# Retention in a written order, with four query blocks inside, padded keys and states, and scores a chunk ahead

## The chip, the cores and the metric

The kernel runs on one core of a Trainium2 chip. The metric is the device time of one execution in microseconds, as the median of several runs. A core has TensorE (PE in the profile), which multiplies matrices and writes to PSUM; VectorE (DVE), ScalarE (ACT) and GpSimd (POOL) for everything else; and SyncE (SP), whose queue issues nearly all DMAs here. Each engine works through its own list of instructions in order and waits on semaphores for the others.

## The reference, cut to what matters

The model is two blocks of two layers each. The change lies in the first layer of the second block, whose mixer splits one projection of the normed input into retention (queries, keys, values), a second attention (stick breaking, with queries `sq`, keys `sk`, values `sv`) and gates. Retention, for 1024 positions, 4 heads of 64 query and key channels and 128 value channels, in 8 chunks of 128:

```
q = rotary(q);  k = rotary(k) * dk ** -0.5
scores  = einsum('bhnid,bhnjd->bhnij', qc, kc) * decay
o_intra = einsum('bhnij,bhnje->bhnie', scores, vc)
chunk_kv = einsum('bhnjd,hj,bhnje->nbhde', kc, k_decay, vc)
step(state, kv): return state * g_chunk + kv, state      # a scan over the chunks
o_inter = einsum('bhnid,hi,nbhde->bhnie', qc, q_decay, r_prev)
out = o_intra + o_inter        # then normalised over each head's 128 channels
```

## The kernel before

All of it is f32. A dense product is three matmuls for each of eight row tiles: weights and activations are split into a high and a low part (`whi`, `wlo`, `ah`, `al`), and high by high, high by low and low by high are added up in PSUM. A block of 128 output channels by 512 positions is 24 matmuls of 512 columns (line 209); the projections that put positions on the partitions (line 221) use 256 columns. A weight block of 256 columns comes in four DMAs of 256 KB into two buffers `wraw`; ScalarE makes `whi`, GpSimd makes `wlo`, and there are two buffers for each of these, so that a block is loaded while the one before it is in use. The retention's own products are plain f32 matmuls; each is two instructions in the trace.

A scheduler orders the instructions of each engine: it goes by the order of the program text, lets later work pass where its simulation finds an engine idle, and `later()` puts work behind all other. PSUM has eight banks of 512 f32 columns: one (`f`) is held for the whole program, and the pool `psum2` of this stage has the other seven, as two double tiles `d` and three single tiles `s`.

`e2` first projects queries and keys of the retention (`both`, 8 blocks in two halves of 512 positions), which VectorE scales on their way out of PSUM (line 1405) and turns by `rope_swap`: four small DMAs that swap halves, a product on GpSimd (L410) and two on VectorE (L411, L412). Then come the values in two blocks (`tok_proj`, emptied by ScalarE, L1371), and `retention`. For each chunk j it computes, on TensorE:

- the scores of four heads, each with 64 rows of the array, the two heads of a tile in separate double-bank halves (L1465); VectorE multiplies them by the decay into `ret_a` (L1467)
- two transposes of the keys (L1472), which VectorE scales into `ret_kt` (L1473)
- for each head the values by `ret_a` (128 rows, L1483) and then, into the same columns, the state `rst` by the scaled queries `ret_q` (64 rows, L1485)
- the new state, two products of 256 columns (L1488), which VectorE adds to the old one, 64 rows by 128 columns at a time (L1493).

ScalarE copies the output over the values (L1497) and squares it (L1499), VectorE sums the squares (L1501). After chunks 3 and 7 VectorE computes 1/sqrt from the sums in nine small steps and scales four chunks (L1509); TensorE transposes them, 16 transposes into four banks (L1514), ScalarE copies each bank out (L1516) and a DMA writes it to `m_scr`.

Behind the retention, under `later()`, come the query, key and value blocks of the second attention (`qkv_proj`): four blocks of `sq`, four of `sk`, then `sv`. The weights of the first two blocks are loaded before the retention ends. One block of `sk` goes to bank `f` and can so be computed inside the retention.

Of the kernel before, what the change touches and what calls it, by code (L numbers as in the profile page):

```python
# [14 lines left out]
AF = mybir.ActivationFunctionType  # L15
ALU = mybir.AluOpType
AX = mybir.AxisListType.X
# [3 lines left out]
P = 128  # L21
# [3 lines left out]
EPS = 1e-6  # L25
# [17 lines left out]
class Kern:  # L43
# [461 lines left out]
    def e1_start(self):  # L505
# [8 lines left out]
        def vectors():  # L514
# [8 lines left out]
            self.silu_c()  # L523
        X, R = {}, {}

# [863 lines left out]
    def e2(self, act):  # L1389
        nc, A, V = self.nc, self.A, self.nc.vector  # L1390
        sq_scr, sk_scr = self.dram("sq_scr", [512, T]), self.dram("sk_scr", [512, T])
        sv_scr, g_scr, m_scr = self.dram("sv_scr", [T, 512]), self.dram("g3_scr", [1024, T]), self.dram("m3_scr", [1024, T])
        self.open_psum("2", "s", d=2, s=3)
        w_in = A["even_w_in_2"]
        sm = self.open("e2s", side="right")
        qp = self.open("retq", side="left")
        cos, sin = self.const("cos_ret", qp), self.const("sin_ret", qp)
        RQ, RK = ([self.t(qp, [P, T], nm=f"r{e}{i}") for i in range(2)] for e in "qk")
        rp = self.open("ret", side="left")

        def rev(lst):
            def evac(i, c, ps):
                a, b = CH[c]
                o = lst[i][:, a:b]
                V.tensor_tensor(o, ps, self.rbc[c], ALU.mult)
                self.rope_swap(rp, o, 2, 32, cos[:, a:b], sin[:, a:b], 512)
            return evac
        self.both(act, (rev(RQ), rev(RK)), self.w_next)
        RV = [self.t(rp, [P, 512], nm=f"rv{j}") for j in range(8)]
        for b in range(2):  # L1410
            self.tok_proj(self.wblk(w_in, 512 + b * 256, 256), act, lambda j: (RV[j][:, b * 256:(b + 1) * 256], None))
# [36 lines left out]
        return mix  # L1448

    def retention(self, rp, RQ, RK, RV, m_scr):  # L1450
# [4 lines left out]
        R = [self.t(rp, [P, P], nm=f"rst{i}") for i in range(2)]  # L1455
        ss, ms, rr = (self.t(rp, [P, 32], nm=n) for n in ("ret_ss", "ret_ms", "ret_r"))
        eo = lambda t: t.rearrange("p (e i x) -> p e i x", e=2, i=4)[:, :, 0:2, :]
        nat = lambda t: t.rearrange("p (i e x) -> p e i x", i=2, e=2)
        col = lambda h: slice((h % 2) * 512 + (h // 2) * P, (h % 2) * 512 + (h // 2) * P + P)
        for j in range(8):  # L1460
            js = slice(j * P, (j + 1) * P)
            s = self.dps()
            for h in range(4):
                r = slice(64 * (h % 2), 64 * (h % 2) + 64)
                mm(s[:, col(h)], RK[h // 2][r, js], RQ[h // 2][r, js], start=True, stop=True)  # L1465
            a = self.t(rp, [P, 512], tag="ret_a", bufs=2)
            V.tensor_tensor(nat(a), eo(s), nat(dec.rearrange("p h i -> p (h i)")), ALU.mult)  # L1467
            if j < 7:
                kt = self.t(rp, [P, 256], tag="ret_kt", bufs=2)
                s = self.sps()  # L1470
# [4 lines left out]
            o = self.dps()  # L1475
            if j:
                qd = self.t(rp, [P, 2, P], tag="ret_q", bufs=2)
                for i in range(2):
                    V.tensor_tensor(qd[:, i], RQ[i][:, js], qdec[:, i], ALU.mult)
            for h in range(4):  # L1480
                hs = slice(h * P, (h + 1) * P)
                r = slice(64 * (h % 2), 64 * (h % 2) + 64)
                mm(o[:, col(h)], a[:, hs], RV[j][:, hs], start=True, stop=j == 0)  # L1483
                if j:
                    mm(o[:, col(h)], qd[r, h // 2], R[h // 2][r], start=False, stop=True)  # L1485
            for i in range(2 if j < 7 else 0):
                d = self.sps()
                mm(d[:, 0:256], kt[:, i * P:(i + 1) * P], RV[j][:, i * 256:(i + 1) * 256], start=True, stop=True)  # L1488
                for e in range(2):
                    r = slice(64 * e, 64 * e + 64)  # L1490
                    kv = d[r, e * P:(e + 1) * P]
                    if j:
                        V.scalar_tensor_tensor(R[i][r], R[i][r], g[2 * i + e], kv, ALU.mult, ALU.add)  # L1493
                    else:
                        V.tensor_copy(R[i][r], kv)
            ot = RV[j]
            nc.scalar.activation(out=nat(ot), in_=eo(o), func=AF.Copy)  # L1497
            sq = self.t(rp, [P, 512], tag="ret_s", bufs=2)
            nc.scalar.activation(out=sq, in_=ot, func=AF.Square)  # L1499
            f = slice(4 * j, 4 * j + 4)  # L1500
            V.reduce_sum(ss[:, f], sq.rearrange("p (h e) -> p h e", h=4), axis=AX)  # L1501
            if j % 4 < 3:
                continue
            f = slice(4 * j - 12, 4 * j + 4)
            V.tensor_scalar(ms[:, f], ss[:, f], 1.0 / P, EPS, ALU.mult, ALU.add)
            self.rsqrt(rr[:, f], ms[:, f], 16)
            for u in range(j - 3, j + 1):
                ov = RV[u].rearrange("p (h e) -> p h e", h=4)
                V.tensor_tensor(ov, ov, rr[:, 4 * u:4 * u + 4].unsqueeze(2).to_broadcast([P, 4, P]), ALU.mult)  # L1509
            c = j // 4  # L1510
            for i in range(4):
                s = self.sps()
                for e in range(4):
                    nc.tensor.transpose(s[:, e * P:(e + 1) * P], RV[c * 4 + e][:, i * P:(i + 1) * P], self.ident)  # L1514
                t = self.stg()
                nc.scalar.activation(out=t, in_=s, func=AF.Copy)  # L1516
                self.dma(m_scr[i * P:(i + 1) * P, c * 512:(c + 1) * 512], t)
# [619 lines left out]
```

## Time and profile before

| | us |
|---|---|
| median of three runs (2606.64, 2608.9, 2610.66) | 2608.9 |
| the profiled execution | 2611.92 |
| its span, first to last instruction on the core | 2610.1 |
| the retention, from its first scores to its last transpose | 1610.78 to 1674.26 |
| four `sq` blocks behind it, up to the first `sk` block in bank `e` | 1674.26 to 1698.20 |

The profile gives, for each engine, the time in which it worked and the share of the span; for TensorE also the granted clock (PEclk, 1.00 is 2.4 GHz, 0.50 is 1.2 GHz). A wait is the idle time just before an instruction and is put down to the instruction that ended it. The start-to-start distance of matmuls is their price; the single times beside them are longer, because matmuls overlap.

### The profile page before, as it was taken

The numbers are of one execution on the slowest core, as the hardware profiler recorded it, in microseconds if no ns is written. First come the engines' busy times: TensorE is split into PE (matmuls) and PEld (weight loads), VectorE is DVE, ScalarE is ACT, GpSimd is POOL, SyncE is SP. The second block draws the span as 40 slices with busy tenths as digits, with TensorE's granted clock in tenths as the row PEclk, the third lists the DMA queues.
The fourth block names the chain that finished last, engine by engine and source line by source line (L and its number), as shares of the span: only waits on it lengthen the run. The fifth ranks groups of instructions, "written<-read, shape, count | busy, mean of one in ns | idle before, by whom it ended". The sixth has DMA issues, their size and how long they took to land.

```text
span 2610.1 us, 36065 instructions
## 1 busy us (share of the span) xinstructions
PE 2446.2 (94%) x12842; PEld 1967.3 (75%) x12842; DVE 1686.4 (65%) x2977; ACT 1118.6 (43%) x2169; POOL 899.0 (34%) x750
## 2 busy tenths in 40 slices
PE   5999999999999989999898989899999999999998
PEld 3887777777678876766576779687877777799888
DVE  6785437787845467777785653347788476673455
ACT  4412226666643225655464322135656333513331
POOL 4214243454411243332321413045552243453231
PEclk7999999999999999999899999899999999999999
DMA  7475431132333222221323522133233332201433
GB/s 239 134 224 190 155 102 56 51 104 74 99 107 124 73 89 61 68 73 54 95 83 97 178 68 72 55 107 106 85 108 119 100 110 89 72 22 54 163 104 101
DMA packets 217092, 265.16 MB, mean 102 GB/s; under 512 B 42768, under 2 KB 142768, under 8 KB 216784
## 3 DMA queue, kind: packets, MB, share of 16 engines
q1 hardware_dynamic: 216192, 262.75, 32.1%
q8 instruction: 101, 1.65, 0.3%
q14 instruction: 79, 0.65, 0.1%
q10 hardware_dynamic: 720, 0.10, 0.0%
HBM read 188.60 MB, written 71.97 MB: 100 GB/s over the span
## 4 chain that ended last, share of the span: by engine, by line
PE 60%; DVE 14%; DMA 10%; issue 8%; ACT 4%; POOL 4%; SPq 1%; DVEq 0%; POOLq 0%; ACTq 0%
PE s L209 9%; PE g L209 6%; PE f L209 4%; PE p L209 4%; PE s L221 4%; PE o L209 2%; DMA wmt<-in_w_modT 2%; PE t L209 2%; PE e L209 2%; PE g L1917 1%; DVE wmj L474 1%; DVE pl L166 1%; DMA mixg<-gate_scr 1%; PE o L1255 1%; PE o L958 1%
## 5 line engine op out<-in xcount | busy, mean ns | idle before, releaser
L166 POOL TENSOR_TENSOR wlo<-wraw,whi 128x512 fp32r<-128x512 f32 (+3 forms) x229 | 317.9, 1400 | 588.2 <-ACT whi L158 526.3
L158 ACT ACTIVATE whi<-wraw 128x512 fp32r<-128x512 f32 (+3 forms) x261 | 154.0, 612 | 359.0 <-PE s L209 82.9
L166 DVE TENSOR_TENSOR pl<-pf,ph 128x512 fp32r<-128x512 f32 (+1 forms) x328 | 254.4, 776 | 79.1 <-ACT pf L953 40.1
L209 PE MATMUL s<-ah,whi 128*128 128x512 f32 (+1 forms) x472 | 190.6, 404 | 13.2 <-DVE hf L1699 3.7
L209 PE MATMUL s<-al,whi 128*128 128x512 f32 (+1 forms) x472 | 189.3, 401 | 2.1 <-DVE al L492 1.4
L209 PE MATMUL s<-ah,wlo 128*128 128x512 f32 (+1 forms) x472 | 189.0, 401 | 0.6 <-POOL wlo L166 0.6
L953 ACT ACTIVATE ph<-s 128x512 fp32r<-128x512 f32 (+1 forms) x176 | 101.4, 576 | 107.5 <-PE s L950 106.7
L915 DVE TENSOR_REDUCE mx<-p 128x1 f32<-128x512 f32 (+1 forms) x208 | 116.9, 575 | 35.1 <-PE p L914 34.1
L1250 ACT ACTIVATE ph<-s 128x512 fp32r<-128x512 f32 x152 | 90.6, 596 | 112.8 <-PE s L1242 59.5
L209 PE MATMUL g<-ah,whi 128*128 128x512 f32 (+1 forms) x312 | 122.2, 392 | 3.2 <-DVE mixg L382 3.2
L209 PE MATMUL g<-ah,wlo 128*128 128x512 f32 (+1 forms) x312 | 121.7, 390 | 0.0
L209 PE MATMUL g<-al,whi 128*128 128x512 f32 (+1 forms) x312 | 121.5, 390 | 0.0
L209 PEld LDWEIGHTS s<-ah,whi 128*128 128x128 f32 x472 | 90.2, 191 | 39.2 <-issue 5.4
L209 PE MATMUL f<-ah,whi 128*128 128x512 f32 x288 | 116.2, 404 | 0.5 <-ACT accq L371 0.5
L209 PE MATMUL f<-ah,wlo 128*128 128x512 f32 x288 | 116.1, 403 | 0.0
L209 PE MATMUL f<-al,whi 128*128 128x512 f32 x288 | 115.8, 402 | 0.0
L209 PEld LDWEIGHTS s<-al,whi 128*128 128x128 f32 x472 | 90.4, 191 | 24.4 <-DVE al L492 2.1
L209 PEld LDWEIGHTS s<-ah,wlo 128*128 128x128 f32 x472 | 90.1, 191 | 22.6 <-issue 1.4
L1588 DVE TENSOR_TENSOR_SCAN scu<-scu,ones_col 128x128 f32<-128x128 f32 (+3 forms) x64 | 97.5, 1537 | 14.3 <-ACT scu L1584 12.3
L1210 DVE CUSTOM_DVE_ANT_0 p<-p,maskt 128x384 f32<-128x384 f32 (+1 forms) x128 | 67.4, 530 | 59.2 <-PE p L1209 59.1
L953 ACT ACTIVATE pf<-s 128x512 f32<-128x512 f32 (+1 forms) x176 | 100.9, 573 | 1.5 <-DVE pl L166 1.4
L474 DVE CUSTOM_DVE_ANT_0 wmj<-wmt,srow,c_b_mod 128x1024 bf16<-128x1024 f32 x56 | 76.8, 1371 | 29.1 <-DMA wmt<-in_w_modT 27.8
(756 smaller groups left out, 7490.5 us busy)
## 6 DMA issues: line engine op xcount, KB each, us to landing
wmt<-in_w_modT SPq DMA_DIRECT2D x32, 512.0 KB
wraw<-in_even_w_in SPq DMA_DIRECT2D x56, 256.0 KB
wraw<-in_odd_w_in SPq DMA_DIRECT2D x48, 256.0 KB
wraw<-in_o_w_in SPq DMA_DIRECT2D x40, 256.0 KB
xold<-x_scr SPq DMA_DIRECT2D x40, 256.0 KB
mraw<-in_w_mod SPq DMA_DIRECT2D x16, 512.0 KB
x_scr<-x SPq DMA_DIRECT2D x32, 256.0 KB
mixx<-m_scr SPq DMA_DIRECT2D x30, 256.0 KB
```

The costliest lines, as they stand in the source:

```text
L158: nc.scalar.activation(out=out, in_=in_, func=AF.Copy)
L166: return e.tensor_tensor(out, in_, hi.bitcast(F32), ALU.subtract)
L209: self.nc.tensor.matmul(out, ws[:, k, c:c + m], a[k][ch], start=first and i == j == 0, stop=last and i == len(ks) - 1 and j == 2)
L221: self.nc.tensor.matmul(out, s[k][ch][:, a:a + P], ws[:, k, c:c + n], start=first and e == i == 0, stop=last and e == len(ks) - 1 and i == 2)
L474: V.tensor_tensor_reduce(out=junk, in0=w, in1=s[:, i], scale=0.5, scalar=self.bm[l][:, m, i:i + 1], op0=ALU.mult, op1=ALU.add, accum_out=s ...
L915: V.reduce_max(mx[:, e, j:j + 1], d[:, 0:y - x], axis=AX)
L953: nc.scalar.activation(out=t, in_=s, func=AF.Exp, scale=MLA_SCALE)
L958: mm(o[0:66, 0:n], vh[:, j, :], ph, start=first, stop=False)
L1210: V.tensor_tensor_reduce(out=d[:, 0:n], in0=d[:, 0:n], in1=self.mask[:, off:off + n], scale=1.0, scalar=-3.0e38, op0=ALU.add, op1=ALU.max, ...
L1250: nc.scalar.activation(out=t, in_=s, func=AF.Exp, scale=0.125)
L1255: mm(o[0:66], vh[:, j, kv, :], ph, start=first, stop=False)
L1588: V.tensor_tensor_scan(out=rev, data0=rev, data1=self.ones.to_broadcast([P, n]), initial=1.0, op0=ALU.mult, op1=ALU.mult)
```

## The change

- The PSUM pool becomes `a`, `o` and `s` with two single tiles each and one `e`; the projections use the seven in turn ("saoe").
- The first weight block of `sq` is loaded in program order, and its four blocks become a generator `beside`, which yields after each row tile (three matmuls, 32 steps in all). `retention` draws from it: 2 steps after the first scores, 3 in every chunk, the rest after the last chunk. `qkv_proj` leaves this block out.
- `in_order` ties each TensorE instruction traced within the retention to the one before it, so that TensorE keeps the order of the text. Other work can still go between.
- Scores: ScalarE copies each key half into a tile `KZ` of two 128-column parts whose other half of the rows is zero (L1478), and the scores use all 128 rows (L1480). They are computed a chunk ahead. The tiles are cleared once on VectorE (L1463).
- States: `rst` has 128 rows by two 128-column parts, with zeros in the other halves; values by `ret_a` come first for all four heads (L1520), and then two products of 256 columns add the states (L1522).
- `norm` stands after chunks 3 and 7 as before; the transposes of the first four chunks come after chunk 5 and those of the last four at the end (`turn`, L1496, L1498).

```
-        self.open_psum("2", "s", d=2, s=3)
+        self.open_psum("2", "s", a=2, o=2, s=2, e=1)
...
-        self.both(act, (rev(RQ), rev(RK)), self.w_next)
+        self.both(act, (rev(RQ), rev(RK)), self.w_next, "saoe")
...
-        self.retention(rp, RQ, RK, RV, m_scr)
+        w, ev = self.wblk(w_in, 1536, 256), self.scaled(sq_scr)
+
+        def beside():
+
+            for c in (0, 1):
+                for i in (0, 1):
+                    yield from self.dense_steps(w, i * P, act, c, "ef", lambda ps: ev(i, c, ps))
+        with self.in_order():
+            self.retention(rp, RQ, RK, RV, m_scr, beside())
...
-                for c0, scr in ((1536, sq_scr), (2048, sk_scr)):
+                for c0, scr in ((1536, sq_scr), (2048, sk_scr))[1 - b:]:
...
-        with self.later():
-            for _ in range(2):
-                next(qkv)
...
+        R = [self.t(rp, [P, 2, P], nm=f"rst{i}") for i in range(2)]
+        KZ = [[self.t(rp, [P, 2, P], nm=f"rkz{b}{i}") for i in range(2)] for b in range(2)]
+        for t in R + KZ[0] + KZ[1]:
+            V.memset(t, 0.0)
...
+        def scores(j):
+            js = slice(j * P, (j + 1) * P)
+            s = self.sps("a")
+            for i in range(2):
+                kz = KZ[j % 2][i]
+                for e in range(2):
+                    r = slice(64 * e, 64 * e + 64)
+                    nc.scalar.activation(out=kz[r, e], in_=RK[i][r, js], func=AF.Copy)
+                for e in range(2):
+                    mm(s[:, (2 * i + e) * P:(2 * i + e + 1) * P], kz[:, e], RQ[i][:, js], start=True, stop=True)
+            A[j] = self.t(rp, [P, 512], tag="ret_a", bufs=2)
+            V.tensor_tensor(A[j], s, dec.rearrange("p h i -> p (h i)"), ALU.mult)
...
+        scores(0)
+        fill(2)
         for j in range(8):
...
             if j < 7:
+                scores(j + 1)
...
+            fill(3)
+            o = self.sps("o")
             for h in range(4):
                 hs = slice(h * P, (h + 1) * P)
-                r = slice(64 * (h % 2), 64 * (h % 2) + 64)
-                mm(o[:, col(h)], a[:, hs], RV[j][:, hs], start=True, stop=j == 0)
-                if j:
-                    mm(o[:, col(h)], qd[r, h // 2], R[h // 2][r], start=False, stop=True)
+                mm(o[:, hs], A[j][:, hs], RV[j][:, hs], start=h == 0, stop=j == 0 and h == 3)
+            for i in range(2 if j else 0):
+                mm(o[:, i * 256:(i + 1) * 256], qd[:, i], R[i].rearrange("p e x -> p (e x)"), start=False, stop=i == 1)
...
+            if j % 4 == 3:
+                norm(j // 4)
+            if j == 5:
+                turn(0)
+        fill(32)
+        turn(1)
```

On TensorE, in the middle of the retention (chunk 3), the list before has the scores of the chunk (`d_16036`, queries by keys), the two key transposes, and then values and state in turn, a pair for each head, of which the first is shown:

```order
L1465 MATMUL d_16036<-rq_3718_15185,rk_3720_15187 128x128 x2
L1465 MATMUL d_16036<-rq_3719_15186,rk_3721_15188 128x128 x2
L1472 MATMUL s_16044<-c_ident,rk_3720_15187 128x128
L1472 MATMUL s_16044<-c_ident,rk_3721_15188 128x128
L1483 MATMUL d_16048<-rv_3741_15467,ret_a_16041 128x128
L1485 MATMUL d_16048<-rst_3774_15930,ret_q_16049 128x128
```

In the list after, TensorE has in the same chunk the end of the three dense steps (`f_16092`, a query block), the values of all four heads, two state products, two products for the new state, and the scores of chunk 5 (`a_16182`):

```order
L209 MATMUL f_16092<-ah_14705,whi_15924 128x512
L209 MATMUL f_16092<-al_14706,whi_15924 128x512
L209 MATMUL f_16092<-ah_14705,wlo_15925 128x512
L1520 MATMUL o_16149<-rv_3741_15467,ret_a_16082 128x128 x4
L1522 MATMUL o_16149<-rst_3780_15948,ret_q_16137 128x256
L1522 MATMUL o_16149<-rst_3781_15949,ret_q_16137 128x256
L1525 MATMUL s_16156<-rv_3741_15467,ret_kt_16132 128x256
L1525 MATMUL s_16160<-rv_3741_15467,ret_kt_16132 128x256
L1480 MATMUL a_16182<-rq_3718_15185,rkz_3784_15952 128x128 x2
L1480 MATMUL a_16182<-rq_3719_15186,rkz_3785_15953 128x128 x2
```

The values and states no longer alternate, and between the scores of a chunk and their use lies a whole chunk.

At the end of the retention TensorE's list before goes from the last values and states (`d_16233`, chunk 7) straight to the transposes of the normalised values `rv`:

```order
L1483 MATMUL d_16233<-rv_3745_15471,ret_a_16231 128x128
L1485 MATMUL d_16233<-rst_3775_15931,ret_q_16234 128x128
L1483 MATMUL d_16233<-rv_3745_15471,ret_a_16231 128x128
L1485 MATMUL d_16233<-rst_3775_15931,ret_q_16234 128x128
L1514 MATMUL s_16263<-c_ident,rv_3742_15468 128x128
L1514 MATMUL s_16271<-c_ident,rv_3742_15468 128x128
L1514 MATMUL s_16279<-c_ident,rv_3742_15468 128x128
```

In the list after, 18 matmuls of the last query block and 24 of a key block (`f_16505`) stand there first; this is the end of the key block on TensorE:

```order
L209 MATMUL f_16505<-ah_14714,wlo_16460 128x512
L209 MATMUL f_16505<-ah_14723,whi_16459 128x512
L1496 MATMUL s_16421<-c_ident,rv_3742_15468 128x128
L209 MATMUL f_16505<-al_14724,whi_16459 128x512
L209 MATMUL f_16505<-ah_14723,wlo_16460 128x512
L1496 MATMUL s_16421<-c_ident,rv_3743_15469 128x128
L1496 MATMUL s_16421<-c_ident,rv_3744_15470 128x128
L1496 MATMUL s_16421<-c_ident,rv_3745_15471 128x128
```

The key block that filled the first chunks before has moved to this place.

On SyncE's queue, ahead of the value projection, the list before has the third part of the value weights (`wraw_15482`) ahead of the rope copies of the first half's queries (`rope_s`):

```order
L128 DMA wraw_15482<-in_even_w_in 128x2x256
L128 DMA rope_s_15218<-rq_3718_15185 32x512 x4
L128 DMA rope_s_15252<-rq_3719_15186 32x512 x4
L128 DMA wraw_15486<-in_even_w_in 128x2x256
L128 DMA wraw_15700<-in_even_w_in 128x2x256
```

In the list after, on the same queue, the third part comes behind these copies and the fourth (`wraw_15486`) behind those of the keys as well:

```order
L128 DMA rope_s_15218<-rq_3718_15185 32x512 x4
L128 DMA rope_s_15252<-rq_3719_15186 32x512 x4
L128 DMA wraw_15482<-in_even_w_in 128x2x256
L128 DMA rope_s_15286<-rk_3720_15187 32x512 x4
L128 DMA rope_s_15320<-rk_3721_15188 32x512 x4
L128 DMA wraw_15486<-in_even_w_in 128x2x256
```

The copies have moved ahead of the weights on the queue.

## Rows read from the trace of the kernel before

**Rows 1.** The page, part 1: busy us, share of the span, instructions
```profile
PE 2446.2 (94%) x12842; PEld 1967.3 (75%) x12842; DVE 1686.4 (65%) x2977; ACT 1118.6 (43%) x2169; POOL 899.0 (34%) x750
```

**Rows 2.** Stretches: us, busy us and count of each engine, PEclk, DMA share
```profile
core 0: us, PE busy (x) PEld busy (x) DVE busy (x) ACT busy (x) POOL busy (x), PEclk, DMA share, GB/s
...
1549.80:1563.60 13.80, 10.74 (x47) 8.49 (x46) 6.16 (x16) 3.01 (x5) 8.67 (x6) 0.88 0.48 136
...
1610.78:1674.26 63.48, 54.80 (x284) 40.82 (x283) 31.75 (x87) 15.96 (x28) 5.05 (x4) 0.85 0.13 42
...
1674.26:1698.20 23.94, 23.11 (x98) 18.26 (x96) 2.83 (x5) 1.73 (x4) 0.67 (x2) 0.98 0.22 82
```

**Rows 3.** TensorE's waits, 1610 to 1675: total us, times, longest
```profile
PE s L1514 <- DVE rv L1509: 4.9, 2, 4.7
...
PE d L1483 <- DVE ret_a L1467: 2.6, 3, 1.1
...
PE s L1488 <- DVE ret_kt L1473: 0.6, 1, 0.6
...
PE s L1514 <- ACT stg L1516: 0.5, 2, 0.3
```

**Rows 4.** Timeline, TensorE: start us, us, line, operation, count
```profile
1612.51 1.05 PE L1483 MATMUL d<-rv,ret_a 128*128 128x128 f32 x8
...
1613.49 0.71 PE L1465 MATMUL d<-rq,rk 64*128 64x128 f32 x8
...
1614.13 1.13 PE L1488 MATMUL s<-rv,ret_kt 128*128 128x256 f32 x4
...
1615.10 0.38 PE L1472 MATMUL s<-c_ident,rk 128*128 128x128 f32 x2
...
1628.06 0.49 PE L1483 MATMUL d<-rv,ret_a 128*128 128x128 f32 x2
...
1628.48 0.48 PE L1485 MATMUL d<-rst,ret_q 64*128 64x128 f32 x2
...
1649.83 1.12 PE L1514 MATMUL s<-c_ident,rv 128*128 128x128 f32 x4 [0.26 <-ACT stg L1516]
...
1650.74 0.63 PE L1472 MATMUL s<-c_ident,rk 128*128 128x128 f32 x2
```

**Rows 5.** Chain of waits in time, 1600 to 1720: start us, us, what
```profile
1710.71 5.61 PE f L209 x24
```

**Rows 6.** Timeline, VectorE, one chunk and the normalisation
```profile
1629.01 0.49 DVE L1479 TENSOR_TENSOR ret_q<-rq,c_ret_qdec 128x128 f32<-128x128 f32 x2 [4.26 <-PE d L1485]
...
1629.63 1.24 DVE L1493 SCALAR_TENSOR_TENSOR rst<-rst,s 64x128 f32<-64x128 f32 x4
...
1630.90 0.69 DVE L1467 TENSOR_TENSOR ret_a<-d,c_ret_dec 128x512 f32<-128x512 f32 x1
...
1631.51 0.41 DVE L1473 TENSOR_TENSOR ret_kt<-s,c_ret_kdec 128x256 f32<-128x256 f32 x1
...
1631.84 0.68 DVE L1501 TENSOR_REDUCE ret_ss<-ret_s 128x4 f32<-128x512 f32 x1
...
1669.66 2.50 DVE L1509 TENSOR_TENSOR rv<-rv,ret_r 128x512 f32<-128x512 f32 x4
```

**Rows 7.** Groups by shape, ScalarE: busy us, mean ns, idle before
```profile
L1271 ACT ACTIVATE gatt<-o 64x256 f32<-64x256 f32 x64 | 24.1, 377 | 1.2
```

**Rows 8.** Stretches of 2 us, columns as in rows 2
```profile
1642.00:1644.00 2.00, 2.00 (x10) 1.55 (x12) 0.00 (x0) 0.00 (x0) 0.00 (x0) 0.50 0.00 0
...
1654.00:1656.00 2.00, 2.00 (x14) 1.45 (x14) 1.07 (x2) 0.38 (x1) 0.00 (x0) 1.00 0.54 189
```

**Rows 9.** TensorE's waits, 1549 to 1611
```profile
PE s L209 <- DVE rq L1405: 2.2, 1, 2.2
...
PE f L369 <- DVE rt L351: 0.9, 1, 0.9
```

**Rows 10.** Timeline, SyncE's queue
```profile
1552.65 5.02 SPq L128 DMA_DIRECT2D rope_s<-rq  x8
```

**Rows 11.** One line, VectorE: ns min/median/max, first and last start
```profile
L511 DVE MEMSET sc<- x1: 272/272/272, 0.9 to 0.9; 128x256 f32 x1
```

More of the change, by code (lines that the diff above doesn't have):

```diff
@@ L1407, in rev @@
             return evac
-        self.both(act, (rev(RQ), rev(RK)), self.w_next)
+        self.both(act, (rev(RQ), rev(RK)), self.w_next, "saoe")
         RV = [self.t(rp, [P, 512], nm=f"rv{j}") for j in range(8)]
         for b in range(2):
-            self.tok_proj(self.wblk(w_in, 512 + b * 256, 256), act, lambda j: (RV[j][:, b * 256:(b + 1) * 256], None))
-        self.retention(rp, RQ, RK, RV, m_scr)
+            self.tok_proj(self.wblk(w_in, 512 + b * 256, 256), act, lambda j: (RV[j][:, b * 256:(b + 1) * 256], None), "saoe")
+        w, ev = self.wblk(w_in, 1536, 256), self.scaled(sq_scr)
[5 more added lines that the diff above has]
+            self.retention(rp, RQ, RK, RV, m_scr, beside())
         def qkv_proj():
             for b in range(2):
-                for c0, scr in ((1536, sq_scr), (2048, sk_scr)):
+                for c0, scr in ((1536, sq_scr), (2048, sk_scr))[1 - b:]:
                     w = self.wblk(w_in, c0 + b * 256, 256)
@@ L1448, in e2, with retention @@
         return mix
-    def retention(self, rp, RQ, RK, RV, m_scr):
+    def retention(self, rp, RQ, RK, RV, m_scr, beside):
         nc, V = self.nc, self.nc.vector
@@ L1454, in retention @@
         g = [float((1.0 - 2.0 ** (-5.0 - h)) ** 128) for h in range(4)]
-        R = [self.t(rp, [P, P], nm=f"rst{i}") for i in range(2)]
+        R = [self.t(rp, [P, 2, P], nm=f"rst{i}") for i in range(2)]
+        KZ = [[self.t(rp, [P, 2, P], nm=f"rkz{b}{i}") for i in range(2)] for b in range(2)]
+        for t in R + KZ[0] + KZ[1]:
+            V.memset(t, 0.0)
         ss, ms, rr = (self.t(rp, [P, 32], nm=n) for n in ("ret_ss", "ret_ms", "ret_r"))
-        eo = lambda t: t.rearrange("p (e i x) -> p e i x", e=2, i=4)[:, :, 0:2, :]
@@ L1458, in retention, with fill @@
-        nat = lambda t: t.rearrange("p (i e x) -> p e i x", i=2, e=2)
-        col = lambda h: slice((h % 2) * 512 + (h // 2) * P, (h % 2) * 512 + (h // 2) * P + P)
+        A = {}
+        def fill(n):
+            for _ in range(n):
+                next(beside, None)
+        def scores(j):
[10 more added lines that the diff above has]
+            V.tensor_tensor(A[j], s, dec.rearrange("p h i -> p (h i)"), ALU.mult)
@@ new lines, in norm, with turn @@
+        def norm(c):
+            f = slice(16 * c, 16 * c + 16)
+            V.tensor_scalar(ms[:, f], ss[:, f], 1.0 / P, EPS, ALU.mult, ALU.add)
+            self.rsqrt(rr[:, f], ms[:, f], 16)
+            for u in range(4 * c, 4 * c + 4):
+                ov = RV[u].rearrange("p (h e) -> p h e", h=4)
+                V.tensor_tensor(ov, ov, rr[:, 4 * u:4 * u + 4].unsqueeze(2).to_broadcast([P, 4, P]), ALU.mult)
+        def turn(c):
+            for i in range(4):
+                s = self.sps("s")
+                for e in range(4):
+                    nc.tensor.transpose(s[:, e * P:(e + 1) * P], RV[c * 4 + e][:, i * P:(i + 1) * P], self.ident)
+                t = self.stg()
+                nc.scalar.activation(out=t, in_=s, func=AF.Copy)
+                self.dma(m_scr[i * P:(i + 1) * P, c * 512:(c + 1) * 512], t)
@@ L1460, in retention @@
+        scores(0)
+        fill(2)
         for j in range(8):
             js = slice(j * P, (j + 1) * P)
-            s = self.dps()
-            for h in range(4):
-                r = slice(64 * (h % 2), 64 * (h % 2) + 64)
-                mm(s[:, col(h)], RK[h // 2][r, js], RQ[h // 2][r, js], start=True, stop=True)
-            a = self.t(rp, [P, 512], tag="ret_a", bufs=2)
-            V.tensor_tensor(nat(a), eo(s), nat(dec.rearrange("p h i -> p (h i)")), ALU.mult)
             if j < 7:
+                scores(j + 1)
@@ L1469, in retention @@
                 kt = self.t(rp, [P, 256], tag="ret_kt", bufs=2)
-                s = self.sps()
+                s = self.sps("s")
                 for i in range(2):
@@ L1474, in retention @@
                                 kdec.unsqueeze(2).to_broadcast([P, 4, 64]), ALU.mult)
-            o = self.dps()
             if j:
@@ L1492, in retention @@
                     if j:
-                        V.scalar_tensor_tensor(R[i][r], R[i][r], g[2 * i + e], kv, ALU.mult, ALU.add)
+                        V.scalar_tensor_tensor(R[i][r, e], R[i][r, e], g[2 * i + e], kv, ALU.mult, ALU.add)
                     else:
-                        V.tensor_copy(R[i][r], kv)
+                        V.tensor_copy(R[i][r, e], kv)
             ot = RV[j]
-            nc.scalar.activation(out=nat(ot), in_=eo(o), func=AF.Copy)
+            nc.scalar.activation(out=ot, in_=o, func=AF.Copy)
             sq = self.t(rp, [P, 512], tag="ret_s", bufs=2)
             nc.scalar.activation(out=sq, in_=ot, func=AF.Square)
[L1500 to L1517, printed above, removed]
+            V.reduce_sum(ss[:, 4 * j:4 * j + 4], sq.rearrange("p (h e) -> p h e", h=4), axis=AX)
+            if j % 4 == 3:
[4 more added lines that the diff above has]
+        turn(1)
     def stick_prep(self, sp, h, sq_scr, sk_scr, sv_scr):
```

3 lines of the change are left out of this document (1 added, 2 removed).

## The prediction, made before the result

> **What bounds the kernel now.** The page comes first. TensorE is busy for 94% of the span, VectorE for 65% [rows 1]; whatever shortens TensorE's own sequence shortens the kernel. So I looked for stretches in which TensorE waits or runs slowly, by the table of stretches. The retention and what follows it up to the end of four query blocks last 63.48 + 23.94 = 87.4 us, and in the first part TensorE is busy for 54.80 of 63.48 us at a mean granted clock of 0.85 [rows 2]. The other engines are busy for half of that part or less, so nothing but the order of the dependent steps holds it. The table of waits names them: 4.9 + 2.6 + 0.6 + 0.5 = 8.6 us, more than half of it one wait of 4.7 us, the last transposes waiting for the normalised values [rows 3]. Before the retention there are two more waits, 2.2 and 0.9 us, where the key and query projections run out of PSUM [rows 9], and the clock there is 0.88 [rows 2].
>
> Behind the retention the two versions have the same instructions in the same order on every engine, from the first key block of the next attention on. So the change is worth what happens between 1549.8 and 1698.2 us, and everything behind it moves as one piece.
>
> **Part 1, the projections before the retention.** Seven banks in turn replace three. The eighth projection block no longer waits for VectorE to empty a bank, and between the sum behind rt and the broadcast that needs rt TensorE now has 35 matmuls in place of 5: 2.2 + 0.9 = 3.1 us go. The clock loss is 13.80 × (1 − 0.88) = 1.7 us [rows 2], most of it behind the longer wait. At most 4.8 us go. Against this stand six clears on VectorE ahead of rt, 6 × 0.27 = 1.6 us [rows 11], hidden behind those 35; SyncE's queue, where the rope copies that took 5.02 us to issue [rows 10] now stand ahead of the third part of the value weights, and the next eight ahead of the fourth; and ScalarE's queue, where the key copies of chunks 0 and 1 wait for the roped keys, with the fourth part's conversion and the emptying of the value blocks behind them. If the value projection gets no further because of these, the gain is 0; the matmuls on the first parts of the weights are put first for five blocks, so I take it as mostly covered: −4, bounds −4.8 and 0.
>
> **Part 2, TensorE's work in the retention.** Prices at full clock come from the timeline, start to start [rows 4]:
> - values alone, 8 instructions of 128 columns in 1613.49 − 1612.51 = 0.98 us: 0.1225 each
> - scores on half the rows, 8 in 0.64 us: 0.08 each
> - 256 columns, 4 in 15.10 − 14.13 = 0.97 us: 0.2425 each
> - values and states in turn, 2 instructions in 28.48 − 28.06 = 0.42 us, where two on whole rows would take 0.245: each change of rows costs some 0.17 us
> - transposes, 4 in 0.91 us at clock 0.5: 0.115 each at full clock
> - a 24-matmul block of the query projection: 5.61 us [rows 5].
>
> After the change, for eight chunks: 64 score instructions on whole rows × 0.1225 = 7.8; 14 key transposes × 0.115 = 1.6; 64 values × 0.1225 = 7.8; 28 state instructions of 256 columns × 0.2425 = 6.8; 28 for the new states = 6.8; 32 transposes of values = 3.7. That is 34.5 us. Padding scores costs 64 × 0.0425 = 2.7 us more than now; padding states saves, as a chunk's values and states take 8 × 0.42 = 3.3 us now and 0.98 + 0.97 = 1.95 then, 1.4 us in each of seven chunks, 9.6 in all. The padded states were not run, and I price them by the nearest row, the 256-column products.
>
> TensorEngine Tiling (Array Packing) in the Trainium skill, Theoretical Speedup, gives up to twice the speed to halves of the rows, which speaks against padding. The score row bears it out in part (0.08 against 0.1225); by the full factor the padded scores would cost 64 × 0.16 = 10.2 us, and the total below would be 2.5 us worse. For the alternating states the row shows no such gain, and the page's Key Properties says that a change of mode drains TensorE.
>
> **Part 3, dense work and what covers what.** Before the common point five blocks are done in both versions (now one inside and four behind; then four inside and one ahead of the last transposes): 5 × 5.61 = 28.0 us. So the work is 34.5 + 28.0 = 62.5 us.
>
> Does TensorE, now held to the written order, wait? In one chunk it has 4.1 us of retention (0.98 + 0.23 + 0.98 + 0.97 + 0.97) and nine dense matmuls, 2.1 us: 6.2 us. VectorE's chunk is 0.49 + 1.24 + 0.69 + 0.41 + 0.68 = 3.5 us [rows 6] and a third of a query emptying. The masked scores are made a chunk ahead; the state update has the scores, the dense matmuls and the values, 4.3 us, to finish 1.24 us. ScalarE's four half copies, at most 0.38 each [rows 7], with the copy and square leave it half idle. No wait in a plain chunk. There remain three places:
> - chunk 5, where VectorE has also normalised (1.9 us of small steps and 2.50 [rows 6]) and 16 transposes share two banks that ScalarE empties: 1.2 us
> - the end: the last f block needs its bank from VectorE, whose emptying stands behind the small steps: 0.8 us
> - the last 16 transposes, again with two banks: 0.6 us. Ahead of their copies ScalarE now has four conversions of the next weights, of which two wait for a DMA; if that lands late, TensorE stands behind it, and the upper bound below has 5 us for that. What waited 4.7 us is now covered by 18 query matmuls and 24 key matmuls, 9.8 us, against about 8 us for the chain of copy, square, sum and normalisation.
>
> Together 2.6 us, bounds 1 and 8. Clock: the first stage lost 63.48 × 0.15 = 9.5 us [rows 2], with the clock at 0.50 behind the short waits [rows 8]; I scale it by the waits, 2.6/8.6, to 2.9 us, bounds 0 and 9.5.
>
> **The sum.** 62.5 + 2.6 + 2.9 = 68.0 us in place of 87.4: −19.4. With part 1, −23.4. The profiled execution took 2611.92 us, 1.8 more than its span and 3.0 more than the median of the three runs, 2608.9; I take the difference from the median: 2585.5.
>
> **Rivals.**
> Smaller gain: the clock falls after the remaining waits as often as it does now (9.5 us lost, waits 5, part 1 worth −2). The clock of 0.50 came with waits of 1 us only, which speaks for it; few such waits remain, which speaks against it. 87.4 − 77 = 10.4, and 2: 2608.9 − 12.4 = 2596.5. Chance 0.2.
> Larger gain: no waits beyond 1 us, no dip, part 1 whole: 87.4 − 63.5 + 4.8 = 28.7, so 2580. Chance 0.12.
> Given back later: the next attention waits for something that TensorE's earlier arrival does not move, and the time stays at 2609. VectorE is busy for much of it, but all its inputs are made behind the common point. Chance 0.03.
> Slower: the granted clock stays at 1.2 GHz for the retention's f32 matmuls, as it did from 1642 to 1644 with TensorE fully busy [rows 8]. If that held for all 34.5 us of them, the stage would take 62.5 + 34.5 + 2.6 = 99.6 us, 12.2 more than now, and part 1 gives 4: 2617. It decides from two thirds of these matmuls on (23 us). Against it: from 1654 to 1656, on such matmuls without any wait, the clock is 1.00. Chance 0.04.
>
> **How the numbers follow.** My forecast has 0.61 and a range of its own, 2581 to 2592. With the larger gain and the smaller one the range is 2578 to 2598; it leaves out 0.1 or somewhat more. This kernel can tell a change of about 0.2%, 5.2 us. Faster by more than that are the forecast, both other gains: 0.93. Within it: the gain given back and an ill form of the slower case: 0.03. Slower: 0.04.
>
> **What would show it.** In the profile after, the retention with its four blocks and the f block should last about 68 us up to the first e block; instructions of the padded scores should start 0.12 us apart and those of the states 0.24; no wait for masked scores; the waits for normalised values gone and none over 1.3 us; the value projection beginning 3 to 5 us earlier. It is wrong if the padded instructions are dearer, if TensorE waits in every chunk for the state update or for ScalarE's key copies, or if PEclk falls under 0.9 over the stage.

## The result, and the profile after

The kernel after took 2575.73 us (median of four runs, 2570.18 to 2578.05) against 2609.19 us of the kernel before in the same series: ratio 0.9861, interval 0.9838 to 0.9884, some 33.5 us faster. The forecast was 2585.5, the range 2578 to 2598: the direction was right, and the gain was larger than the range allowed for. The profiled execution has a span of 2576.2 us, 33.9 less than that of before.

Three marks divide the span into four pieces that have the same work in both: the first matmul of the projections behind `rt` (the normalisation's 1/sqrt factors, made on VectorE), the first scores, and the first `sk` block in bank `e`, from where both do the same.

| us | before | after | difference |
|---|---|---|---|
| span up to the projections | 1508.57 | 1504.91 | −3.7 |
| projections, up to the first scores | 102.21 | 98.24 | −4.0 |
| stage: retention and five dense blocks | 87.43 | 63.00 | −24.4 |
| from there to the end | 911.89 | 910.05 | −1.8 |

The page's first part for the kernel after, to be held against [rows 1]:

```profile
PE 2428.7 (94%) x12814; PEld 1962.3 (76%) x12814; DVE 1681.6 (65%) x2983; ACT 1126.9 (44%) x2201; POOL 895.3 (35%) x750
```

TensorE is busy for 17.5 us less, though it has only 28 instructions fewer; the other half of the gain is idle time that went. Stretches of the kernel after, columns as in [rows 2]; the first is the end of the query and key projections, the second the whole stage (its window opens 0.05 us early):

```profile
1545.80:1556.40 10.60, 10.60 (x52) 8.68 (x51) 3.71 (x17) 1.15 (x2) 4.08 (x3) 1.00 0.20 50
...
1603.10:1666.15 63.05, 60.74 (x352) 52.07 (x351) 35.89 (x92) 26.00 (x57) 10.16 (x8) 1.00 0.23 73
```

In [rows 2] the stage is 63.48 + 23.94 us, with TensorE busy for 77.9 of them at clocks of 0.85 and 0.98. Now it is one stretch in which TensorE works for 60.74 of 63.05 us, with the granted clock at 1.00, that is 2.4 GHz, all through. TensorE's waits in that stage, against [rows 3]:

```profile
PE f L209 <- DVE stg L1361: 0.8, 1, 0.8
PE e L209 <- ACT stg L1498: 0.7, 1, 0.7
PE s L1496 <- ACT stg L1498: 0.5, 2, 0.3
PE s L1496 <- DVE rst L1530: 0.4, 1, 0.4
```

(An f or e block is a dense block that adds up in bank `f` or `e`.) No wait for masked scores, none for normalised values, none in a plain chunk. The waits before the stage, against [rows 9]:

```profile
PE s L209 <- DVE rt L351: 1.5, 1, 1.5
PE s L209 <- DVE al L1309: 0.4, 1, 0.4
```

Those of rows 9 are gone. These two were there before as well (1.7 and 0.7 us). TensorE's timeline over one chunk, against [rows 4]:

```profile
1613.60 1.05 PE L1520 MATMUL o<-rv,ret_a 128*128 128x128 f32 x8
1614.49 1.03 PE L1522 MATMUL o<-rst,ret_q 128*128 128x256 f32 x4
1615.36 1.03 PE L1525 MATMUL s<-rv,ret_kt 128*128 128x256 f32 x4
1616.22 1.05 PE L1480 MATMUL a<-rq,rkz 128*128 128x128 f32 x8
1617.11 0.38 PE L1509 MATMUL s<-c_ident,rk 128*128 128x128 f32 x2
1617.25 0.48 PE L209 MATMUL f<-ah,whi 128*128 128x512 f32 x1
```

Start to start: values 0.89 us for eight (0.111 each; 0.1225 in the prediction), padded states 0.87 for four and new states 0.86 (0.217 each; 0.2425), padded scores 0.89 for eight, key transposes 0.14 for two. VectorE in the same chunk, against [rows 6], at unchanged durations:

```profile
1615.99 1.23 DVE L1530 SCALAR_TENSOR_TENSOR rst<-rst,s 64x128 f32<-64x128 f32 x4
1617.31 0.69 DVE L1482 TENSOR_TENSOR ret_a<-a,c_ret_dec 128x512 f32<-128x512 f32 x1
```

State and masked scores are done at 1617.2 and 1618.0; TensorE comes to the next values at 1619.43, behind nine dense matmuls.

### The profile page after: what moved, and what is told of

The parts are those of the page before. It is cut to its first block, busy times and chain, and to the rows that moved or that the text cites. A ratio compares the mean times of both kernels' runs of the same rounds, so it can differ in the third digit from the quotient of the medians.

```text
span 2576.2 us, 36051 instructions
## 1 busy us (share of the span) xinstructions
PE 2428.7 (94%) x12814; PEld 1962.3 (76%) x12814; DVE 1681.6 (65%) x2983; ACT 1126.9 (44%) x2201; POOL 895.3 (35%) x750
## 5 line engine op out<-in xcount | busy, mean ns | idle before, releaser
L209 PE MATMUL s<-ah,whi 128*128 128x512 f32 (+1 forms) x392 | 159.3, 406 | 12.2 <-DVE hf L1725 5.9
L209 PE MATMUL s<-al,whi 128*128 128x512 f32 (+1 forms) x392 | 158.0, 403 | 1.8 <-DVE al L492 1.4
L209 PE MATMUL s<-ah,wlo 128*128 128x512 f32 (+1 forms) x392 | 157.4, 402 | 0.0
L915 DVE TENSOR_REDUCE mx<-p 128x1 f32<-128x512 f32 (+1 forms) x208 | 116.7, 574 | 34.5 <-PE p L914 33.5
L209 PE MATMUL f<-ah,whi 128*128 128x512 f32 x304 | 123.2, 405 | 1.3 <-DVE stg L1361 0.8
L209 PE MATMUL f<-ah,wlo 128*128 128x512 f32 x304 | 122.8, 404 | 0.0
L209 PE MATMUL f<-al,whi 128*128 128x512 f32 x304 | 122.8, 404 | 0.0
L209 PEld LDWEIGHTS s<-ah,whi 128*128 128x128 f32 x392 | 75.3, 192 | 34.2 <-DVE hf L1725 6.8
L209 PEld LDWEIGHTS s<-al,whi 128*128 128x128 f32 x392 | 75.4, 192 | 20.6 <-DVE al L492 2.1
L1250 ACT ACTIVATE pf<-s 128x512 f32<-128x512 f32 x152 | 90.1, 593 | 0.1
```

Of the source, the lines that this page charges most:

```text
L209: self.nc.tensor.matmul(out, ws[:, k, c:c + m], a[k][ch], start=first and i == j == 0, stop=last and i == len(ks) - 1 and j == 2)
L915: V.reduce_max(mx[:, e, j:j + 1], d[:, 0:y - x], axis=AX)
L1250: nc.scalar.activation(out=t, in_=s, func=AF.Exp, scale=0.125)
```

## The experiments

Each was run beside the kernel before on the same chip. For the reasons I go by the stage's length in the profile, which repeats far better than the total, and hold the totals beside it.

**The same two kernels again.** No edit.

> The changed kernel once more. From the two profiles, 28.4 us of the 33.9 us lie in the stretch that the change touches (first query and key projections to the first e block), 3.7 ahead of it and 1.8 behind it, where the instructions are the same. Theory A (chance): the stretches outside differ from execution to execution by some 3 us; this profile has the stage at 63 us again, but the start of the projections moves by 1 to 4 us, and the gain over five rounds is 28 to 31 us. Theory B (the change also shortens what is outside, for instance through other addresses): the start of the projections stays near 1505 us, and the gain is 33 us or more.

> The kernel before once more, for its profile. Theory A: the start of the projections differs from 1508.6 us by 1 to 4 us, and the stage has its 87 us within 2. Theory B: the start is at 1508 to 1509 again. The clock in the stage (0.85) should fall again behind the short waits.

> The changed kernel a third time, beside the others. By chance alone (theory A), stage 63.0 us again within 0.1, projections 97 to 99 us, the stretches outside anywhere within 3 us, and the gain over the kernel before between 28 and 33 us. Theory B (something outside gains as well) would put it at 33 us or more.

The first repeat gave 2578.6 us (ratio 0.9893, 0.9878 to 0.9907), the second 2574.34 (0.9883, 0.9863 to 0.9903). The stage of the kernel after took 63.00, 63.01 and 62.99 us in its three profiles, that of the kernel before 87.43 and 87.42 in two: −24.4 us, to some hundredths. The projections took 98.24, 97.09 and 95.74 against 102.21 and 104.15: −4 to −8, in the mean −6.2. Ahead of them every kernel here but one (the unpadded one below, whose banks move work across this mark) has TensorE's instructions in the same order, and still they began between 1502.4 and 1511.6 us; the piece behind the stage took 904 to 913. So a gain of 24.4 + 6.2 = 30.6 us repeats; it lies in the intervals of both repeats (28.1 and 32.3 us by medians) and at the lower end of the first series' interval. In the first pair of profiles 5.5 of the 33.9 us lie outside the changed region. What makes those outer pieces wander was not found.

**Which part of the padding and grouping counts.** Four forms of the states: alternating with the values on all 128 rows; alternating on 64 rows, unpadded, with the scores still padded; values first and then states on 64 rows; and nothing padded at all, the 64-row scores right behind the 64-row states. The three unpadded ones use a double bank for `o`, and so other banks in the projections.

```
# alternating, 128 rows                    (e_alt128)
+ if j: mm(o[:, hs], qd[:, h // 2], R[h // 2][:, h % 2], start=False, ...)   # behind each head's values
# alternating, 64 rows                     (e_alt64)
+ if j: mm(o[:, col(h)], qd[r, h // 2], R[h // 2][r, h % 2], start=False, ...)
# values first, then 64 rows               (e_grp64)
+ for h in range(4 if j else 0):
...
+     mm(o[:, col(h)], qd[r, h // 2], R[h // 2][r, h % 2], start=False, ...)
# as e_grp64, scores unpadded and moved behind the states, query blocks begun with bank f   (e_half)
+ mm(s[:, col(h)], RK[h // 2][r, js], RQ[h // 2][r, js], start=True, stop=True)
...
+ if j < 7:
+     scores(j + 1)
```

> Values and padded states in turn for each head, all on 128 rows, as 56 single products of 128 columns in place of 28 of 256; the rest is the changed kernel. Theory of the rows (what the alternation cost before was the change between 128 and 64 rows): the products start 0.11 us apart as they do now, stage within 0.5 us of 63.0. Rival (it is the alternation itself, that is, a new sum into the same columns right behind the last one): 0.15 us more at each of 8 steps in seven chunks, stage 70 to 73 us.

> States without padding: the output has two banks for the two halves of rows, and values (128 rows) and states (64 rows) come in turn as before the change; scores stay padded and a chunk ahead, the dense work stays inside; the projections take five banks. Theory of the rows: 3.3 us for a chunk's values and states in place of 1.8, stage 63.0 + 7 x 1.5 = 73.5 us, granted clock near 1.00, since TensorE does not wait longer; whole kernel slower than the change by 8 to 12 us. Rival A (the alternation cost nothing once dense work stands beside it): stage 63 to 65. Rival B (products on 64 rows themselves let the clock fall): PEclk under 0.95 in the stage, 76 us or more.

> States without padding as in the one before, but the four values first and then the four states on 64 rows, two halves of the rows in two banks. Theory of the rows: only one change of rows in a chunk instead of eight, states 8 x 0.08 = 0.64 us and 0.1 to 0.2 for the change, against 0.87 now: stage 62 to 64 us. Rival (padding itself is what gains): stage 66 us or more.

> The change without any padding: scores and states on 64 rows with two banks each, the scores of the next chunk right behind the states (so that both are done between two changes of rows), dense work inside as in the change, its banks begun with f so that the last key block need not wait 0.8 us for one. Theory of the rows: a chunk has 0.89 + 0.65 + 0.65 + 0.86 us and two changes of some 0.1 us in place of 0.89 + 0.87 + 0.89 + 0.86: stage 63.0 - 8 x 0.2 - 0.8 = 60 to 61.5 us. Rival (padding is what the stage needs): 64 us or more. The whole kernel should be equal to the change within what can be told.

| | stage, us | TensorE busy | total, us | ratio to before |
|---|---|---|---|---|
| after (padded, grouped) | 63.00 | 60.69 | 2575.73 | 0.9861 (0.9838 to 0.9884) |
| alternating, 128 rows | 63.22 | 60.9 | 2574.27 | 0.9855 (0.9832 to 0.9878) |
| alternating, 64 rows | 74.01 | 71.71 | 2589.71 | 0.9924 (0.9907 to 0.9941) |
| grouped, 64 rows | 62.83 | 60.53 | 2579.67 | 0.9882 (0.9853 to 0.991) |
| nothing padded | 66.78 | 60.15 | 2582.49 | 0.9913 (0.989 to 0.9935) |

TensorE's timeline of the alternating 64-row kernel, dense matmuls left out:

```profile
1627.86 0.38 PE L1524 MATMUL q<-rv,ret_a 128*128 128x128 f32 x2
1628.17 0.49 PE L1526 MATMUL q<-rst,ret_q 64*128 64x128 f32 x2
1628.59 0.49 PE L1524 MATMUL q<-rv,ret_a 128*128 128x128 f32 x2
1629.01 0.48 PE L1526 MATMUL q<-rst,ret_q 64*128 64x128 f32 x2
...
1631.09 1.13 PE L1529 MATMUL s<-rv,ret_kt 128*128 128x256 f32 x4
1632.05 1.05 PE L1483 MATMUL a<-rq,rkz 128*128 128x128 f32 x8
```

And the grouped 64-row one:

```profile
1621.30 1.05 PE L1524 MATMUL q<-rv,ret_a 128*128 128x128 f32 x8
1622.28 0.71 PE L1527 MATMUL q<-rst,ret_q 64*128 64x128 f32 x8
1622.93 1.13 PE L1530 MATMUL s<-rv,ret_kt 128*128 128x256 f32 x4
1623.90 1.05 PE L1483 MATMUL a<-rq,rkz 128*128 128x128 f32 x8
```

In turn, two instructions take 0.42 us (1628.17 to 1628.59), where two on whole rows take 0.22; values, states and new states of a chunk take 4.19 us (1627.86 to 1632.05). Grouped they take 2.60, padded 2.62. So seven chunks cost 1.57 × 7 = 11.0 us more when they alternate on different rows, which is what the stage shows (74.01 − 63.00). Alternation on the same rows costs next to nothing (63.22 us, at 0.22 us for two instructions); it is the change of rows that is dear:

```profile
1619.32 0.38 PE L1520 MATMUL o<-rv,ret_a 128*128 128x128 f32 x2
1619.54 0.39 PE L1522 MATMUL o<-rst,ret_q 128*128 128x128 f32 x2
1619.76 0.39 PE L1520 MATMUL o<-rv,ret_a 128*128 128x128 f32 x2
```

And padding the states is not what pays: the grouped 64-row states take 0.65 in place of 0.87 us, and the products that border on them 0.98 and 0.97 in place of 0.89 and 0.86, which evens out. The Trainium skill (TensorEngine Tiling (Array Packing), Key Properties) says that a change of the tiling mode drains TensorE; these rows agree in that each change costs time (0.42 us for two instructions in place of 0.22), and give it a size.

The kernel with nothing padded is busy for 0.5 us less than after, and 3.8 us slower in the stage. Its waits there:

```profile
PE s L1506 <- DVE rst L1531: 4.0, 4, 2.9
PE s L1494 <- ACT stg L1496: 1.1, 2, 0.8
```

The key transposes (L1506) now come behind the new states and find both `s` banks still being read. The 60 to 61.5 us expected for it failed on such waits: TensorE is idle for 6.6 us in place of 2.3. They point at the changed order and not at the half rows, but unpadded scores in the order of after were not run. The half rows themselves are quick where they stand side by side, states and then scores, eight in 0.55 and eight in 0.54 us, 0.068 each:

```profile
1611.72 0.71 PE L1521 MATMUL q<-rst,ret_q 64*128 64x128 f32 x8
1612.27 0.61 PE L1478 MATMUL d<-rq,rk 64*128 64x128 f32 x8
1612.81 1.13 PE L1526 MATMUL s<-rv,ret_kt 128*128 128x256 f32 x4
```

Its six runs spread from 2573.53 to 2590.39, so the total says little.

**Only the grouping, in the kernel before.** The values of all heads first, then the four 64-row states; the rest is the kernel before.

```
-                mm(o[:, col(h)], a[:, hs], RV[j][:, hs], start=True, stop=j == 0)
-                if j:
-                    mm(o[:, col(h)], qd[r, h // 2], R[h // 2][r], start=False, stop=True)
+                mm(o[:, col(h)], a[:, hs], RV[j][:, hs], start=h < 2, ...)
+            for h in range(4 if j else 0):
...
+                mm(o[:, col(h)], qd[r, h // 2], R[h // 2][r], start=False, stop=h > 1)
```

> The kernel before with one edit: a chunk's four products with the values first and then its four with the state, in place of one and one for each head; no padding, no dense work inside, the scheduler's order otherwise. Theory (alternation and uncovered waits are two separate costs): seven chunks x 1.5 us = 11 us less, stage 76 to 78 us. Rival (what TensorE saves comes back as waits for VectorE and a lower clock): stage 82 us or more.

It took 2593.35 us (2592.18 to 2596.18; ratio 0.9955, 0.9939 to 0.997), and its stage 73.43: −14.0, more than the 11.0 of the last experiment. TensorE's idle time did not shrink (9.5 us before, 10.2 here); the clock changed. Stretches of the kernel before (columns as in rows 2), the middle of the retention and the whole stage:

```profile
1630.78:1652.78 22.00, 18.33 (x78) 13.28 (x78) 10.28 (x30) 3.94 (x7) 0.00 (x0) 0.69 0.11 40
1610.78:1698.20 87.42, 77.92 (x379) 59.08 (x378) 34.58 (x92) 17.69 (x31) 5.72 (x6) 0.88 0.16 53
```

The same of the grouped kernel:

```profile
1622.41:1646.41 24.00, 19.67 (x155) 15.62 (x156) 17.92 (x51) 7.85 (x14) 0.00 (x0) 1.00 0.19 67
1606.41:1679.84 73.43, 63.22 (x379) 50.15 (x379) 34.43 (x92) 17.59 (x31) 5.74 (x6) 0.95 0.18 63
```

The longest waits in those middle stretches (the idle time in brackets), in the kernel before:

```profile
1631.74 0.46 PE L1483 MATMUL d<-rv,ret_a 128*128 128x128 f32 x2 [0.70 <-DVE ret_a L1467]
1639.49 0.46 PE L1483 MATMUL d<-rv,ret_a 128*128 128x128 f32 x2 [1.09 <-DVE ret_a L1467]
1645.73 0.79 PE L1483 MATMUL d<-rv,ret_a 128*128 128x128 f32 x2 [0.79 <-DVE ret_a L1467]
```

And in the grouped kernel:

```profile
1624.16 1.13 PE L1483 MATMUL d<-rv,ret_a 128*128 128x128 f32 x8 [0.70 <-DVE ret_a L1467]
1629.15 1.13 PE L1483 MATMUL d<-rv,ret_a 128*128 128x128 f32 x8 [1.30 <-DVE ret_a L1467]
1632.42 1.16 PE L1483 MATMUL d<-rv,ret_a 128*128 128x128 f32 x8 [1.04 <-DVE ret_a L1467]
...
1651.71 2.82 PE L1515 MATMUL s<-c_ident,rv 128*128 128x128 f32 x12 [4.71 <-DVE rv L1510]
```

Idle shares of 17% and 18% (3.67 of 22 us, 4.33 of 24), waits of about the same length; yet at the one place the mean clock is 0.69, at the other it stays at 1.00; it falls to 0.50 only behind the wait of 4.71, the last line. With the alternating 64-row kernel (no long waits, clock 1.00 throughout) this makes a table of two by two of the stage:

| us (granted clock) | alternating on 64 rows | values and states grouped |
|---|---|---|
| dense blocks behind, waits uncovered | 87.43 (0.88) | 73.43 (0.95) |
| dense blocks inside, waits covered | 74.01 (1.00) | 62.83 to 63.00 (1.00) |

Each change is worth 10.4 to 11.2 us where the other has been made, and 3 us more (14.0 and 13.4) where it has not. The rows differ in more than the place of the dense blocks: the lower one also has the written order, padded scores and the scores a chunk ahead; the next experiment bears on these. With waits of up to 1.3 us the middle stretch ran at 1.2 GHz only where waits and alternation came together. By what rule the chip decides this the runs don't tell.

**The dense blocks all ahead.** The four query blocks before the first scores, none inside.

```
+        fill(32)
         scores(0)
-        fill(2)
...
-            fill(3)
...
-        fill(32)
         turn(1)
```

> All four query blocks are computed ahead of the first scores, none inside; padding, scores a chunk ahead and the written order stay. Theory of the waits: TensorE now waits in each chunk for VectorE's masked scores or state update, 0.5 to 1.5 us, and 3 to 5 us at the end, 8 to 14 us in all, and the clock falls as it did before: slower than the change by 12 to 25 us, stage 75 to 88 us. Rival (the padding and the order of the scores did it, the dense work inside is worth little): slower by under 5 us, clock near 1.00.

It took 2584.61 us (ratio 0.992, 0.9902 to 0.9937). Projections and blocks together last 120.82, the stage 52.04: 172.9 in place of 158.7 to 161.2 in three profiles of after, some 12 to 14 us more. The total shows less, 6.0 us against the first repeat (2578.6, beside which it ran); the profiled execution (2591.47) was the slowest of its four, so the size is known to a factor of two. The stage, and its waits:

```profile
1630.66:1682.70 52.04, 43.00 (x255) 37.56 (x253) 31.80 (x89) 23.75 (x52) 5.04 (x4) 0.86 0.19 67
```

```profile
PE s L1496 <- DVE rv L1490: 5.1, 3, 4.8
PE s L1496 <- DVE rst L1529: 3.1, 1, 3.1
```

The same matmuls at the wrong place let 8.2 us of waits return, to the transposes after chunk 5 and at the end, and the clock falls to a mean of 0.86 with them. In the plain chunks no wait returns, so the dense matmuls are not needed there; the written order and the scores a chunk ahead do it. But without dense work inside, written order, padding and lead gain nothing on top of the grouping that this profile shows: with 97.0 us for the projections (the mean of the three profiles) stage and blocks take 75.8 here, no less than the 73.43 of the grouped kernel before.

**Three banks for the projections.**

```
-        self.both(act, (rev(RQ), rev(RK)), self.w_next, "saoe")
+        self.both(act, (rev(RQ), rev(RK)), self.w_next, "sse")       # and the same for tok_proj
```

> The projections ahead of the retention take three banks in turn, as before the change, in place of seven; all else stays. Theory: the wait of 2.2 us for a bank comes back, with the clock's fall behind it: slower than the change by 3 to 5 us, all of it ahead of the first scores. Rival (the 4 us came from the rope copies ahead of the weights on SyncE's queue, not from banks): no difference of more than 1 us.

The projections take 104.61 us in place of 95.7 to 98.2, the stage 62.99. The total, 2582.62 (ratio 0.9895, 0.9868 to 0.9922), can't be told from that of after. TensorE's waits there:

```profile
PE f L369 <- DVE rt L351: 3.3, 1, 3.3
...
PE s L209 <- DVE rq L1405: 1.4, 1, 1.4
```

The two waits of rows 9 are back, 4.7 us, and with them all that the projections had gained. So the banks carry part 1; whether the reordered queues add a little can't be told. The wait for `rt` is 3.3 us and not the 0.9 of before: the six clears (1.64 us) now stand in VectorE's way to `rt`. With seven banks TensorE has work for that time.

**Scores in their own chunk.**

```
-        scores(0)
...
+            scores(j)
             if j < 7:
-                scores(j + 1)
```

> Each chunk's scores are computed in that chunk, ahead of its three dense steps, in place of a chunk ahead; the rest is the changed kernel. Theory (the dense steps, 2.1 us, cover the masking of 0.7 us, so the lead is worth nothing): stage 63 to 64 us. Rival (without the lead the values wait for the masked scores): 0.5 to 1 us in each chunk, stage 67 to 71 us, with waits for ret_a in the table.

The stage takes 62.92 us by the mark, the total 2577.88 (ratio 0.9876, 0.9859 to 0.9893). But the mark has moved: the first six dense matmuls now come ahead of the first scores. Counted from the start of the last value product to the first `sk` block in bank `e`, it takes 65.26 us (from 1601.95) against 63.12 in after (from 1603.03), 2.1 us more. Two waits are new, one for bank `e`, which the value projection has just left, and one in chunk 5, behind the normalisation on VectorE:

```profile
1602.78 0.50 PE L209 MATMUL e<-ah,whi 128*128 128x512 f32 x1 [0.56 <-ACT rv L1371]
...
1636.99 1.13 PE L1519 MATMUL o<-rv,ret_a 128*128 128x128 f32 x8 [1.07 <-DVE ret_a L1482]
```

In the plain chunks the lead is worth nothing: nine dense matmuls between scores and values cover VectorE's mask as well. In chunk 5 and at the start it is worth some 2 us.

## Why the prediction came out too small

The mechanism held, and three terms of the sum were mis-sized. The step that failed most is the clock, scaled by the waits: 2.9 us forecast, 0 measured. The prices of whole-row products were 1.8 us too high in sum, and part 1 was put at −4 where the profiles show −6.2 in the mean. The first total lies outside the range partly by chance: with the 30.6 us that repeat it would have been 2578.3, just inside.

- **What bounds the kernel**: right. TensorE's own sequence in this stage was the limit, and nearly all of the repeatable gain was taken in the two stretches named.
- **Given back later, and the slower case**: neither came. The padded matmuls ran at 2.4 GHz, and the 911.9 us behind the stage stayed at 910.
- **Part 1**: −4 was forecast, with −4.8 as the end; the first pair shows −4.0, the repeats −6.2 in the mean. The two waits went as foretold. Idle time there went from 3.75 to 0.45 us in the first pair, as forecast; the rest is clock, which varies between executions in both kernels (102.21 us at a mean of 0.97, 104.15 at 0.94; after 98.24 at 0.97, 95.74 at 1.00). I had one profile, and the end of the bounds was too near. SyncE's and ScalarE's reordered queues cost nothing that shows: the value projection (L221) does not appear among the waits.
- **Waits in the stage**: 2.6 forecast, 2.3 measured: 0.35 + 0.23 behind chunk 5 (1.2 forecast), 0.78 for the last f block (0.8), 0.25 and then 0.69 ahead of the `e` block (0.6). The conversions ahead of ScalarE's copies held nothing up.
- **The clock**: the step that failed. I scaled the loss of 9.5 us by the waits to 2.9, and it was 0, with the granted clock at 1.00 all through. Waits are not a measure of it: the grouped kernel before kept them all and kept full clock through the middle. Also, 9.5 was too much to begin with, since it counted the idle time inside the stretch. TensorE's busy time in the stage fell from 77.92 to 60.69, 17.2 us; 11.2 of that is the alternation at full clock (71.71 − 60.53), so the clock had cost about 6.
- **The work**: 62.5 us forecast, 60.69 of busy time measured. The prices of whole-row products in rows 4 were taken beside 64-row ones, and each such border adds about 0.1 us (eight values 0.98 there, 0.89 without). I took them for the plain price, so values, scores, states and new states came out some 10% too dear, 2.9 us together, of which the other items took back about 1. The 9.6 us that padding the states was to save came as 11, from the grouping. And padding the scores cost almost nothing: with their borders, values, scores and new states took 0.98 + 0.64 + 0.97 = 2.59 us on 64-row scores [rows 4] and take 0.89 + 0.89 + 0.86 = 2.64 now, 0.4 us over eight chunks in place of 2.7.
- **The sum**: the stage came to 63.0, not 68.0: 2.9 by the clock, 1.8 by the work, 0.3 by the waits. The larger-gain rival had the mechanism (no dip: 63.5 us) and too small a chance. The remaining misfit of the first total, some 3 us, is the wander of the outer pieces; a range around a gain must have room for it.
- **What the text ascribed**: it priced padded states as a gain of their own. The padding is not needed: grouped states on 64 rows do as well (62.83 us). Scores a chunk ahead are worth some 2 us, and not in the plain chunks. What pays is that values and states are grouped, that dense matmuls stand where TensorE waited, and, ahead of the stage, the banks.

## What to carry to other kernels

Group TensorE's products by how many rows they use before thinking of padding: alternating forms cost some 0.2 us at each change, and in a stretch that also waits they cost clock on top. Price an instruction only from a stretch whose neighbours have its own shape. And place independent dense work where the trace shows a wait; the same work ahead of the stage gave back 6 (by the totals) to 14 (by the profile) of 31 us.

## What the runs showed of the hardware that was not expected

- f32 instructions of 128 columns, two on 128 rows and two on 64 in turn, take 0.42 us for every two; eight and eight in groups take 0.98 + 0.65 us, borders included. In turn on the same rows every two take 0.22 us, and there is no cost.
- 64-row products in two halves ran at 0.068 us side by side and at 0.08 between whole-row ones, which take 0.111: 1.6 and 1.4 times as fast. The Trainium skill (TensorEngine Tiling (Array Packing), Theoretical Speedup) gives up to twice; no run here reached it, and the borders took back the rest: 62.83 us for the stage on grouped 64 rows, 63.00 padded.
- Waits of 0.7 to 1.3 us left the granted clock at 1.00 in one kernel and went with 0.50 in another that differs only in the order of values and states. Waits of 2.9 to 4.8 us were followed by 0.50 with grouped values too.
